# First layer of a hybrid mixer: normalisation applied after the transpose instead of before it

## Chip, cores and metric

The kernel runs on one core of one Trainium2 chip. The metric is the device time of one execution in microseconds (us); three runs of the kernel before have a median of 1519.49 (1518.29 to 1520.88). The engines are called by their short names: PE (TensorE, matrix products and transposes), DVE (VectorE), ACT (ScalarE), POOL (GpSimd) and SP (SyncE, which here only issues transfers).

## The reference

Two layers of a diffusion backbone over 512 tokens x and 256 context tokens, 1024 channels each. A layer normalises its tokens, modulates them with a scale and a shift that are products of a condition vector with a weight, projects the result h to 3840 channels for four mixers, and merges the mixers. The change concerns only how h of the first layer is made:

```python
def rmsnorm(x, gain):
    xf = x.astype(jnp.float32)
    y = xf * lax.rsqrt(jnp.mean(xf * xf, axis=-1, keepdims=True) + EPS)
    return (y * gain.astype(jnp.float32)).astype(x.dtype)
...
    for l in range(DEPTH):
        shift, scale, gate = jnp.split((silu_c @ w_mod[l] + b_mod[l])[:, None, :], 3, axis=-1)
        shift_c, scale_c, gate_c = jnp.split(silu_cc @ w_mod[l] + b_mod[l], 3)
        h = rmsnorm(x, norm_gain[l]) * (1.0 + scale) + shift
        hc = rmsnorm(xc, norm_gain[l]) * (1.0 + scale_c) + shift_c
        za, zb, zh, zf, zg = jnp.split(h @ w_in[l], SPLIT_IDX, axis=-1)
```

## The kernel before, in words

The 768 tokens (512 + 256) lie as six tiles of 128. For the projections, h is needed transposed: channels on partitions, 8 blocks of 128 channels by 768 tokens. Each fp32 value is held as a high part that PE multiplies at its fast rate and a low remainder (`h_hi`, `h_lo`; for weights `wh`, `wl`), and each product is three: high by high, high by low, low by high. The helper `split` makes such a pair: ACT rounds to the high part, DVE subtracts.

The function `opening` makes `h_hi` and `h_lo` of layer 0. The tokens come in eight transfers of 384 KB, `x[j, u]`: three token tiles (u = 0 or 1) by 256 channels (j = 0 to 3). ACT squares each, DVE sums the squares, and `rstd` forms the reciprocal root mean square by an integer first guess and three rounds of refinement, 13 tiny DVE instructions, once for u = 0 and once for u = 1. DVE scales the tokens in place, PE transposes them into two PSUM buffers (`psw`), and ACT copies the transposed blocks out. The modulation comes in eight pieces of 1 MB of `w_mod`, taken in four steps i, each with the shift piece i and the scale piece 4 + i for two of the eight blocks. For a piece, `mod_rows` multiplies the condition with it (`spread`, 16 instructions on PE, at 32 output rows), ACT copies the rows out (`mrow`), and `columns` turns them into per-channel columns with four PE instructions and one DVE copy; `mod_columns` adds bias and gain. Then DVE applies scale and shift to the blocks and `split` writes `h_hi` and `h_lo`.

The other stream is `Weights`: projection weights arrive in pieces of 512 KB in two raw buffers (`wraw`), ACT and DVE split them into `wh` and `wl` (four buffers each), and every pair of pieces serves one projection. The first projection, `hg_gates`, gives the forget gates of the recurrent mixer (HGRN2). Its four results (two halves of 128 columns, two ranges of 384 tokens) stand in two `psw` buffers, and its products are cut into groups of two channel blocks.

No order is written by hand. Every operation is recorded first; `Program.order` then plays the program with a price for each operation and issues, engine by engine, the one that could start earliest by these prices, ties going to the lower rank. Weight transfers and weight splits have their rank lowered by `AHEAD` (400). The engines then run their instructions strictly in that order, so an instruction that waits holds what stands behind it on its engine. All compute instructions have one line in the profile, L345, where the order is emitted; the tiles tell them apart.

Of the kernel before, what the change touches and what calls it, by code (L numbers as in the profile page):

```python
# [21 lines left out]
P = 128  # L22
# [3 lines left out]
NT = NX + NC  # L26
# [17 lines left out]
LEVELS = (64, 32, 16, 8, 4, 2, 1)  # L44
# [119 lines left out]
AHEAD = 400  # L164
# [185 lines left out]
def tile_hybrid_mixers(ctx, tc, io, out, dump=None):  # L350
# [6 lines left out]
    nc = Program()  # L357
# [21 lines left out]
    def psg():  # L379
        return pg.tile([P, 512], F32, tag="g", name=nm("psg"))  # L380
# [25 lines left out]
    def transpose(out, in_):  # L406
        nc.tensor.transpose(out, in_, ident)
# [6 lines left out]
    ident = kc[:, KC_ID:KC_ID + P]  # L414
    blk = kc[:, KC_BLK:KC_BLK + P]
    csel = kc[:, KC_SEL:KC_SEL + 2]
    rsel = [kc[:, KC_SEL + 2 + w:KC_SEL + 3 + w].to_broadcast([P, P]) for w in range(2)]
    masks = cpool.tile([P, len(LEVELS), P], I8, name="masks")

    hi_t = hpool.tile([P, 8, NT], F32R, tag="hhi", name="h_hi")  # L420
    lo_t = hpool.tile([P, 8, NT], F32R, tag="hlo", name="h_lo")

    def load_masks():
        for a, b in ((0, 4), (4, len(LEVELS))):
            mraw = slot([P, b - a, P], I32)
            nc.gpsimd.dma_start(mraw, io["masks"][:, a:b, :])
            nc.vector.tensor_copy(masks[:, a:b, :], mraw)


    sides, done, flags = [], set(), set()  # L430
# [33 lines left out]
    def rsqrt(v, n, size=None):  # L464
        small = lambda _, *a: _small(size or n, *a)[:, 0:n]
        i = small(n, "ri", 1, I32)
        nc.vector.tensor_scalar(i, v.bitcast(I32), 1, None, ALU.logical_shift_right)
        y0 = small(n, "ry", 1, I32)
        ts(y0, i, -1.0, RSQRT_MAGIC)
        y = y0.bitcast(F32)  # L470
        t = small(n, "rt", 1)
        for k in range(3):
            tt(t, y, y, ALU.mult)
            stt(t, t, -0.5, v, ALU.mult, ALU.mult)
            z = small(n, "rz", 3)
            stt(z, t, 1.5, y, ALU.add, ALU.mult)
            y = z
        return y

    def split(hi, lo, src):  # L480
        act(hi, src)
        tt(lo, src, hi.bitcast(F32), ALU.subtract)

    class Weights:
# [5 lines left out]
            self.raw, self.ready, self.work = [], [], None  # L490
            self.held = self.current = 0

        def fetch(self):
            while self.plan and len(self.raw) + bool(self.work) < RAW_BUFS:
                t = wpool.tile([P, 1024], F32, tag="wraw", bufs=RAW_BUFS, name=nm("wraw"))
                nc.ahead = AHEAD
                nc.sync.dma_start(t, self.plan.pop(0))
                nc.ahead = 0
                self.raw.append(t)
# [68 lines left out]
    weights = Weights(plan())  # L568
# [53 lines left out]
            nc.sync.dma_start(t[-1][:, 0:n, :], src[:, 256 * a:256 * (a + n)].rearrange("p (k c) -> p k c", c=256))  # L622
        return lambda k: t[k // 3][:, k % 3, :]

    def mod_rows(w):
        ps = psg()[:, 0:256]
        spread(ps, w, range(8))
        rows = sp.tile([P, 256], F32, tag="mrow", bufs=2, name=nm("mrow"))
        act(rows, ps)
        return rows  # L630

    def columns(tmp, j, rows):
        ps = psg()[:, 0:4]
        for b in range(2):
            mm(ps[:, 2 * b:2 * b + 2], rows[:, P * b:P * (b + 1)], csel)
        nc.vector.tensor_copy(tmp[:, j // 4, 2 * (j % 4):2 * (j % 4) + 2, :], ps.rearrange("p (k w) -> p k w", w=2))
# [10 lines left out]
    def opening():  # L647


        mc = cpool.tile([P, 2, 8, 2], F32, tag="modc", bufs=1, name=nm("modc"))  # L650
        tmp = small(32, "mt", 1).rearrange("p (a k w) -> p a k w", a=2, w=2)
        norm = Norm(None)
        x = {}
        for u in range(2):
            for j in range(4):
                x[j, u] = slot([P, 3, 256])
                nc.sync.dma_start(x[j, u], io["xin"][384 * u:384 * (u + 1), 256 * j:256 * (j + 1)].rearrange("(t p) d -> p t d", p=P))
        fetch = lambda i: [mod_fetch(io["w_mod"][0, j]) for j in (4 + i, i)]
        w = {0: fetch(0)}
        weights.fetch()  # L660
        for u in range(2):
            for j in range(4):
                sq = slot([P, 3, 256])
                act(sq, x[j, u], AF.Square)
                nc.vector.tensor_reduce(norm.ss[:, 3 * u:3 * u + 3, j], sq, AX.X, ALU.add)
            r = norm.rstd(3 * u, 3 * u + 3, 4)
            for j in range(4):
                tt(x[j, u], x[j, u], r.unsqueeze(2).to_broadcast([P, 3, 256]), ALU.mult)
        w[1] = fetch(1)
        xT = []  # L670
        for i in range(4):
            for k in (2 * i, 2 * i + 1):
                ps = psw()[:, 0:NT]
                for t in range(6):
                    transpose(ps[:, P * t:P * (t + 1)], x[i, t // 3][:, t % 3, P * (k % 2):P * (k % 2 + 1)])
                xT.append(slot())
                act(xT[k], ps)
        for i in range(4):
            for j, wj in zip((4 + i, i), w.pop(i)):
                columns(tmp, j, mod_rows(wj))  # L680
            mod_columns(0, mc, tmp, 2 * i, 2 * i + 2)
            for k in (2 * i, 2 * i + 1):
                for c, n0, n1 in ((0, 0, NX), (1, NX, NT)):
                    ts(xT[k][:, n0:n1], xT[k][:, n0:n1], mc[:, 0, k, c:c + 1], mc[:, 1, k, c:c + 1])
                split(hi_t[:, k, :], lo_t[:, k, :], xT[k])
            if i < 2:
                w[i + 2] = fetch(i + 2)
                for _ in range(4):
                    weights.pump()
# [35 lines left out]
    class Norm:  # L725
# [8 lines left out]
            act(junk, x, AF.Square, accum_out=self.ss[:, t, j:j + 1])  # L734

        def rstd(self, t0, t1, n):
            v = small(3, "sv", 1)
            m = t1 - t0
            nc.vector.tensor_reduce(v[:, 0:m], self.ss[:, t0:t1, 0:n], AX.X, ALU.add)
            ts(v[:, 0:m], v[:, 0:m], 1.0 / D, EPS)  # L740
            return rsqrt(v[:, 0:m], m, 3)

        def scale(self, t0, t1, n):

# [504 lines left out]
    def hg_mix(l, z, res):  # L1249
        full = l == 0  # L1250
        W = NT if full else NX
        nch = W // P
        yield from wait_for((l, "hf", 0))
        if full:
            load_masks()
        fl, om, dl = hg_bounds(l)
        gn = small(64, "hgn", 1)
        nc.gpsimd.dma_start(gn, io["smalls"][l:l + 1, SM_HGG:SM_HGG + 64].partition_broadcast(P).rearrange("p a d -> p (a d)"))
# [264 lines left out]
    mc = None  # L1523
# [80 lines left out]
def _constants():  # L1604
# [13 lines left out]
            kc[r, KC_SEL + w] = 1.0  # L1618
            kc[r, KC_SEL + 2 + w] = 0.5
    i = np.arange(P)  # L1620
    masks = np.zeros((P, len(LEVELS), P), np.int32)
    for n, L in enumerate(LEVELS):
        same = (i[:, None] // (2 * L)) == (i[None, :] // (2 * L))
        masks[:, n] = same & ((i[:, None] // L) != (i[None, :] // L))
# [85 lines left out]
```

## Time and profile before

| | us |
|---|---|
| median of three runs | 1519.49 |
| the profiled execution | 1520.19 |
| its span, first to last instruction | 1518.4 |
| PE busy in the span | 1457.1 |
| DVE busy | 953.6 |
| ACT busy | 628.5 |
| POOL busy | 106.7 |

A row of the timeline starts with the start in us from the beginning of the span and a duration; "x4" merges four like instructions, and the duration then runs from the first start to the last end. A row by forms gives, behind the bar, the busy time in us, the mean of one instruction in ns, and the idle time before them. A product is named by its output and inputs, the moving shape last: `psw<-h_hi,wh 128*128 128x384` is one of the three products of a weight tile with 384 tokens. Successive products overlap: they show 0.34 us each and start 0.17 apart. The granted clock of PE (PEclk) has two levels, 1.00 for 2.4 GHz and 0.50 for 1.2 GHz; a value between is a mean over both.

### The profile page before, as it was taken

Reading aid. Unit: us, or ns where it says so; the run is one execution under the profiler, and the core shown is the slowest. Engines: PE = TensorE matmul, PEld = TensorE weight load, DVE = VectorE, ACT = ScalarE, POOL = GpSimd, SP = SyncE. Lnnn points to the kernel's source line nnn. Section 1 sums busy time; section 2 is a strip of 40 time slices with the busy share of each in tenths; the row PEclk is TensorE's granted clock in tenths of the full one; section 3 lists DMA queues with packets and bytes.
Section 4 is the critical chain, followed back from the end, with each engine's and each line's share of the span. In section 5 each row is a group of like instructions: output and inputs, shape, how many; then the busy total and the mean of one; then the engine's idle time right before and its main releaser. Section 6 shows DMA issues by size and latency. Waiting matters only on the chain.

```text
span 1518.4 us, 25432 instructions
## 1 busy us (share of the span) xinstructions
PE 1457.1 (96%) x10068; PEld 1331.9 (88%) x10068; DVE 953.6 (63%) x2058; ACT 628.5 (41%) x1384; POOL 106.7 (7%) x207
## 2 busy tenths in 40 slices
PE   3999999999999997999999999999999999999998
PEld 2899989889999997889999999898887889888788
DVE  7794988577553355643444467979967855673544
ACT  5344454466522243431323244436445634552330
POOL 1000002210000010100001110000131000110000
PEclk9999999999999998999999999999999999999999
DMA  9211012332322142362222331211253222545332
GB/s 350 109 43 43 32 57 70 85 85 91 115 77 70 53 107 93 75 218 74 80 73 92 113 103 57 70 33 56 70 134 98 88 83 84 136 132 176 101 111 74
DMA packets 50599, 144.76 MB, mean 95 GB/s; under 512 B 7280, under 2 KB 12400, under 8 KB 50480
## 3 DMA queue, kind: packets, MB, share of 16 engines
q1 hardware_dynamic: 38336, 112.21, 22.7%
q0 software_dynamic: 12144, 30.93, 8.0%
q8 instruction: 79, 1.29, 0.3%
q14 instruction: 40, 0.33, 0.1%
HBM read 123.98 MB, written 4.19 MB: 84 GB/s over the span
## 4 chain that ended last, share of the span: by engine, by line
PE 85%; DVE 6%; ACT 5%; issue 2%; DMA 1%; SPq 0%; ACTq 0%; DVEq 0%; POOLq 0%
PE psg L345 69%; PE psw L345 11%; PE pst L345 4%; DVE u L345 3%; ACT u L345 3%; DVE sm L345 2%; ACT wh L345 1%; DMA u<-in_xin_dram 1%; ACT mth L345 0%; DVE wl L345 0%; DMA u<-in_rpb_dram 0%; DVE nss L345 0%; DVE psw L345 0%; SPq L345 0%; ACT h_hi L345 0%
## 5 line engine op out<-in xcount | busy, mean ns | idle before, releaser
L345 PE MATMUL psg<-h_hi,wh 128*128 128x384 f32 (+2 forms) x1216 | 439.6, 362 | 4.0 <-ACT mth L345 2.8
L345 PE MATMUL psg<-h_lo,wh 128*128 128x384 f32 (+2 forms) x1216 | 430.3, 354 | 0.2 <-DVE h_lo L345 0.2
L345 PE MATMUL psg<-h_hi,wl 128*128 128x384 f32 (+2 forms) x1216 | 430.4, 354 | 0.0
L345 DVE TENSOR_TENSOR wl<-wraw,wh 128x512 fp32r<-128x512 f32 x312 | 201.7, 686 | 175.8 <-ACT wh L345 174.9
L345 ACT ACTIVATE wh<-wraw 128x512 fp32r<-128x512 f32 x312 | 180.2, 624 | 244.7 <-PE psg L345 218.7
L345 PEld LDWEIGHTS psg<-h_hi,wh 128*128 128x128 f32 x1216 | 230.1, 189 | 24.9 <-ACT mth L345 5.7
L345 PEld LDWEIGHTS psg<-h_hi,wl 128*128 128x128 f32 x1216 | 229.8, 189 | 15.8
L345 PEld LDWEIGHTS psg<-h_lo,wh 128*128 128x128 f32 x1216 | 230.4, 189 | 14.8 <-DVE h_lo L345 0.5
L345 PE MATMUL psg<-wh,h_hi 128*128 128x256 f32 x544 | 156.3, 287 | 0.0
L345 PE MATMUL psw<-u,u 64*128 64x128 f32 (+6 forms) x1144 | 141.2, 299 | 12.3 <-ACT u L345 7.5
L345 PE MATMUL psg<-wl,h_hi 128*128 128x256 f32 x544 | 151.0, 278 | 0.0
L345 PE MATMUL psg<-wh,h_lo 128*128 128x256 f32 x544 | 150.9, 277 | 0.0
L345 ACT ACTIVATE u<-psw 128x768 f32<-128x768 f32 (+12 forms) x248 | 114.4, 485 | 81.3 <-PE psw L345 72.7
L345 PEld LDWEIGHTS psw<-u,u 64*128 64x128 f32 (+2 forms) x1144 | 113.1, 192 | 28.3 <-ACT u L345 13.2
L345 ACT ACTIVATE u<-psw,sm 128x768 f32<-128x768 f32 (+2 forms) x120 | 90.6, 758 | 88.9 <-DVE sm L345 75.7
L345 PE MATMUL psg<-wh,u 128*128 128x256 f32 x640 | 114.2, 280 | 0.9 <-ACT mth L345 0.9
L345 ACT ACTIVATE mth<-psg 128x384 f32<-128x384 f32 (+1 forms) x120 | 62.1, 519 | 127.8 <-PE psg L345 120.4
L345 DVE SCALAR_TENSOR_TENSOR mth<-mth,psg 128x384 f32<-128x384 f32 (+1 forms) x96 | 57.1, 595 | 91.0 <-ACT mth L345 73.9
L345 PE MATMUL psg<-u,wh 128*128 128x384 f32 (+1 forms) x384 | 107.6, 361 | 0.2 <-DVE u L345 0.2
L345 DVE TENSOR_REDUCE sm<-psw 128x1 f32<-128x768 f32 (+3 forms) x100 | 89.5, 901 | 26.1 <-PE psw L345 25.6
L345 PEld LDWEIGHTS psg<-wh,h_hi 128*128 128x128 f32 x544 | 102.2, 188 | 4.0
L345 POOL DMA_DIRECT2D u<-u x132 | 65.1, 505 | 568.8 <-ACT u L345 343.0
(128 smaller groups left out, 2002.9 us busy)
## 6 DMA issues: line engine op xcount, KB each, us to landing
wraw<-in_w_merge_dram SPq DMA_DIRECT2D x64, 512.0 KB, 3.6
wraw<-in_w_in_dram SPq DMA_DIRECT2D x60, 512.0 KB, 3.8
u<-in_w_mod_dram SPq DMA_DIRECT2D x32, 384.0 KB, 7.0
wraw<-in_w_up_dram SPq DMA_DIRECT2D x16, 512.0 KB, 3.5
wraw<-in_w_out_dram SPq DMA_DIRECT2D x16, 512.0 KB, 4.2
u<-u POOLq DMA_DIRECT2D x72, 96.0 KB, 2.4
u<-in_w_gate_dram SPq DMA_DIRECT2D x16, 384.0 KB, 6.3
u<-u POOLq DMA_DIRECT2D x24, 192.0 KB, 2.6
```

Source lines behind the costliest of these rows:

```text
L345: getattr(getattr(nc, engine), method)(*map(f, args), **{k: f(v) for k, v in kw.items()})
```

## The change

Tokens arrive ordered by channel range (j outside, u inside), the first two weight pieces come behind the first two modulation pieces (`weights.fetch(0)` leaves the rank alone), and the masks come as int8 in one transfer without a conversion. The tokens are transposed unscaled, DVE copies the blocks out, and ACT squares five of the eight transfers in narrow pieces with an accumulator. `rstd` is called once for all six tiles; a diagonal tile `dg` of the six columns, multiplied by a tile of ones, gives `R`, a row over the 768 tokens on all partitions. One SCALAR_TENSOR_TENSOR multiplies a block by scale and `R`, ACT adds the shift while it rounds to `h_hi`, and a second SCALAR_TENSOR_TENSOR adds the shift and subtracts `h_hi`. All modulation rows share one PSUM buffer, `pm`.

```diff
+    nc.gpsimd.dma_start(masks, io["masks"])
-    def load_masks():
-        for a, b in ((0, 4), (4, len(LEVELS))):
-            mraw = slot([P, b - a, P], I32)
-            nc.gpsimd.dma_start(mraw, io["masks"][:, a:b, :])
-            nc.vector.tensor_copy(masks[:, a:b, :], mraw)
...
-        weights.fetch()
-        for u in range(2):
-            for j in range(4):
-                sq = slot([P, 3, 256])
-                act(sq, x[j, u], AF.Square)
-                nc.vector.tensor_reduce(norm.ss[:, 3 * u:3 * u + 3, j], sq, AX.X, ALU.add)
-            r = norm.rstd(3 * u, 3 * u + 3, 4)
-            for j in range(4):
-                tt(x[j, u], x[j, u], r.unsqueeze(2).to_broadcast([P, 3, 256]), ALU.mult)
+        weights.fetch(0)
         w[1] = fetch(1)
         xT = []
-        for i in range(4):
-            for k in (2 * i, 2 * i + 1):
+        for j in range(4):
+            for u in range(2):
+                if 2 * j + u < 5:
+                    for t in range(3):
+                        norm.square(3 * u + t, j, x[j, u][:, t, :])
+                else:
+                    sq = slot([P, 3, 256])
+                    act(sq, x[j, u], AF.Square)
+                    nc.vector.tensor_reduce(norm.ss[:, 3 * u:3 * u + 3, j], sq, AX.X, ALU.add)
+            for k in (2 * j, 2 * j + 1):
...
-                act(xT[k], ps)
+                nc.vector.tensor_copy(xT[k], ps)
+        r = norm.rstd(0, 6, 4)
+        dg, ones, R = slot([P, 6, P]), slot([P, P]), slot()
+        nc.vector.memset(ones, 1.0)
+        tt(dg, ident.unsqueeze(1).to_broadcast([P, 6, P]), r.unsqueeze(2).to_broadcast([P, 6, P]), ALU.mult)
+        ps = psw()
+        mm(ps[:, 0:512], ones, dg[:, 0:4, :])
+        mm(ps[:, 512:768], ones, dg[:, 4:6, :])
+        act(R, ps[:, 0:NT])
+        pm = pst()
         for i in range(4):
             for j, wj in zip((4 + i, i), w.pop(i)):
-                columns(tmp, j, mod_rows(wj))
+                columns(tmp, j, mod_rows(wj, pm[:, 0:256]), pm[:, 256 + 4 * j:260 + 4 * j])
...
-                    ts(xT[k][:, n0:n1], xT[k][:, n0:n1], mc[:, 0, k, c:c + 1], mc[:, 1, k, c:c + 1])
-                split(hi_t[:, k, :], lo_t[:, k, :], xT[k])
+                    h, hi, lo = xT[k][:, n0:n1], hi_t[:, k, n0:n1], lo_t[:, k, n0:n1]
+                    stt(h, h, mc[:, 0, k, c:c + 1], R[:, n0:n1], ALU.mult, ALU.mult)
+                    act(hi, h, AF.Identity, bias=mc[:, 1, k, c:c + 1])
+                    stt(lo, h, mc[:, 1, k, c:c + 1], hi.bitcast(F32), ALU.add, ALU.subtract)
```

What the new recording does to the order is seen at three places. On DVE, before, near the end of the normalisation: `nss` holds the sums of squares, `sm` the columns of `rstd`, u_81 to u_91 are tokens.

```order
L345 TENSOR_REDUCE nss_141<-u_205 128x3
L345 TENSOR_TENSOR u_81<-u_81,sm_211 128x768
L345 TENSOR_TENSOR u_85<-u_85,sm_211 128x768
L345 TENSOR_TENSOR u_87<-u_87,sm_211 128x768
L345 TENSOR_TENSOR u_91<-u_91,sm_211 128x768
L345 TENSOR_REDUCE nss_141<-u_215 128x3
L345 TENSOR_REDUCE sm_230<-nss_141 128x3
```

On DVE now, at the same place; the COPY rows bring transposed blocks out of PSUM, u_214, u_239 and u_256 are the three wide squares.

```order
L345 COPY u_212<-psw_197 128x768
L345 TENSOR_REDUCE nss_110<-u_214 128x3
L345 COPY u_235<-psw_218 128x768
L345 COPY u_237<-psw_228 128x768
L345 TENSOR_REDUCE nss_110<-u_239 128x3
L345 TENSOR_REDUCE nss_110<-u_256 128x3
L345 COPY u_272<-psw_241 128x768
L345 TENSOR_REDUCE sm_274<-nss_110 128x6
```

The scalings are gone from between the reduces, and copies of blocks that were transposed unscaled stand there. On PE before, at the start of the first projection (`psw_491<-h_hi,wh_105`), behind the columns (`kc,mrow`) and the last spread (`u,cst`):

```order
L345 MATMUL psg_462<-kc,mrow_459 128x2 x2
L345 MATMUL psg_467<-kc,mrow_465 128x2 x2
L345 MATMUL psg_474<-u_189,cst 32x256 x3
L345 MATMUL psg_474<-u_232,cst 32x256 x3
L345 MATMUL psg_474<-u_239,cst 32x256 x2
L345 MATMUL psw_491<-h_hi,wh_105 128x384
L345 MATMUL psw_491<-h_lo,wh_105 128x384
L345 MATMUL psw_491<-h_hi,wl_110 128x384
```

On PE now, at the start of the same projection (`psw_368<-h_hi,wh_314`):

```order
L345 MATMUL pst_259<-u_136,cst 32x256 x3
L345 MATMUL pst_259<-u_147,cst 32x256 x3
L345 MATMUL pst_259<-u_151,cst 32x256 x2
L345 MATMUL psw_368<-h_hi,wh_314 128x384
L345 MATMUL psw_368<-h_lo,wh_314 128x384
L345 MATMUL psw_368<-h_hi,wl_320 128x384
...
L345 MATMUL pst_259<-kc,mrow_365 128x2 x2
L345 MATMUL pst_259<-u_153,cst 32x256 x3
L345 MATMUL pst_259<-u_164,cst 32x256 x3
L345 MATMUL pst_259<-u_170,cst 32x256 x2
```

The first products came behind the spreads of all eight pieces; now they come behind the third, and the other spreads stand between products. On DVE now, between the third and the fourth step; `wl_504`, `wl_523` and `wl_557` are low parts of weight pieces, `sm_303` the columns, `modc_341` the scale and shift:

```order
L345 TENSOR_TENSOR wl_504<-wraw_329,wh_492 128x512 x2
L345 SCALAR_TENSOR_TENSOR h_lo<-u_237,modc_341,h_hi 128x256
L345 TENSOR_TENSOR wl_523<-wraw_338,wh_515 128x512 x2
L345 COPY sm_303<-pst_259 128x4 x2
L345 TENSOR_TENSOR wl_557<-wraw_519,wh_547 128x512 x2
L345 TENSOR_TENSOR sm_303<-sm_303,cols 128x2x4
L345 SCALAR_TENSOR_TENSOR modc_341<-sm_303,cols 128x4
L345 COPY modc_341<-sm_303 128x4
L345 SCALAR_TENSOR_TENSOR u_272<-u_272,modc_341,u_334 128x512
```

Three pairs of low weight parts, the second to the fourth of which were not there before, stand ahead of the fourth step (u_272).

## Rows read from the trace of the kernel before

**Rows 1.** The page, 40 slices of the span, busy tenths of PE.
```profile
PE   3999999999999997999999999999999999999998
```
**Rows 2.** Table by stretches: us, busy time and instructions of each engine, clock, DMA.
```profile
0.00:48.00 48.00, 23.34 (x204) 15.12 (x204) 34.77 (x91) 24.21 (x38) 5.66 (x14) 0.96 0.95 340
48.00:100.00 52.00, 52.00 (x372) 50.17 (x370) 44.26 (x67) 19.45 (x35) 0.00 (x0) 0.97 0.12 41
```
**Rows 3.** Waits of PE: for whom, us in total, times, longest.
```profile
PE psg L345 <- DVE sm L345: 19.4, 1, 19.4
```
**Rows 4.** The chain that ended last, opening: start, us, what.
```profile
20.67 3.47 DVE u L345 x4
...
29.72 3.05 PE psw L345 x15
```
**Rows 5.** Timeline of PE, first products of the first two projections.
```profile
48.01 0.69 PE L345 MATMUL psw<-h_hi,wh 128*128 128x384 f32 x1
...
66.62 0.34 PE L345 MATMUL psg<-h_hi,wh 128*128 128x384 f32 x1
```
**Rows 6.** Timeline of ACT: the tanh, and a square with accumulator (layer 1).
```profile
6.82 0.22 ACT L345 ACTIVATE sm<-cols 128x16 f32<-128x16 f32 x1 [0.66 <-DMA cols<-in_cols_dram]
...
838.20 0.42 ACT L345 ACTIVATE sq<-u 128x256 f32<-128x256 f32 x1 [2.95 <-DVE u L345]
838.52 0.18 ACT L345 ACTIVATION_READ_ACCUMULATOR sq<-u 128x1 f32 x1
```
**Rows 7.** DVE by forms, whole span: busy us, mean ns, idle before.
```profile
L345 DVE TENSOR_REDUCE sm<-psw 128x1 f32<-128x768 f32 x64 | 60.4, 953 | 18.0 <-PE psw L345 17.9
L345 DVE TENSOR_TENSOR h_lo<-u,h_hi 128x768 fp32r<-128x768 f32 x8 | 7.4, 956 | 0.9 <-ACT h_hi L345 0.7
L345 DVE SCALAR_TENSOR_TENSOR mth<-mth,u 128x512 f32<-128x512 f32 x8 | 5.5, 690 | 0.1
L345 DVE TENSOR_SCALAR u<-u,modc 128x512 f32<-128x512 f32 x8 | 4.4, 544 | 0.1
L345 DVE SCALAR_TENSOR_TENSOR u<-u,sm,u 128x256 f32<-128x256 f32 x8 | 3.8, 480 | 0.1
L345 DVE TENSOR_SCALAR u<-u,modc 128x256 f32<-128x256 f32 x8 | 3.3, 408 | 0.0
L345 DVE SCALAR_TENSOR_TENSOR sm<-sm,sm 128x3 f32<-128x3 f32 x12 | 1.9, 160 | 0.3
```
**Rows 8.** ACT by forms, whole span.
```profile
L345 ACT ACTIVATE u<-psw 128x768 f32<-128x768 f32 x46 | 37.2, 811 | 24.0 <-PE psw L345 22.0 <-DVE u L345 1.6
L345 ACT ACTIVATE u<-u 128x768 f32<-128x768 f32 x37 | 31.3, 845 | 19.8 <-DVE u L345 14.9 <-DMA u<-in_xin_dram 4.1 <-DVE masks L345 0.3
```
**Rows 9.** PE: a spread and columns (timeline); fp32 products by form.
```profile
37.50 1.07 PE L345 MATMUL psg<-u,cst 128*32 128x256 f32 x16
39.21 0.51 PE L345 MATMUL psg<-kc,mrow 128*128 128x2 f32 x4
...
L345 PE MATMUL psg<-mrow,kc 128*128 128x256 f32 x24 | 6.5, 379 | 0.0
```
**Rows 10.** Table by stretches of 1 us; the clock is third from the end.
```profile
28.00:29.00 1.00, 0.00 (x0) 0.00 (x0) 0.86 (x6) 0.00 (x0) 0.00 (x0) 1.00 1.05 405
31.00:32.00 1.00, 1.00 (x7) 0.92 (x6) 1.00 (x2) 1.00 (x3) 0.00 (x0) 0.50 1.04 390
```
**Rows 11.** The page's DMA issues (KB, us to landing), and SP's timeline.
```profile
wraw<-in_w_in_dram SPq DMA_DIRECT2D x60, 512.0 KB, 3.8
u<-in_w_mod_dram SPq DMA_DIRECT2D x32, 384.0 KB, 7.0
...
20.94 14.68 SPq L345 DMA_DIRECT2D u<-in_w_mod_dram  x16
```
**Rows 12.** Timeline of DVE and PE where the recurrent mixer starts.
```profile
60.38 0.56 DVE L345 TENSOR_SCALAR u<-psw 128x384 f32<-128x384 f32 x1 [1.52 <-PE psw L345]
...
85.14 0.94 PE L345 MATMUL psw<-u,u 64*128 64x128 f32 x12
```

More of the change, by code (lines that the diff above doesn't have):

```diff
@@ L491, in __init__, with fetch @@
             self.held = self.current = 0
-        def fetch(self):
+        def fetch(self, ahead=AHEAD):
             while self.plan and len(self.raw) + bool(self.work) < RAW_BUFS:
                 t = wpool.tile([P, 1024], F32, tag="wraw", bufs=RAW_BUFS, name=nm("wraw"))
-                nc.ahead = AHEAD
+                nc.ahead = ahead
                 nc.sync.dma_start(t, self.plan.pop(0))
@@ L623, in mod_fetch, with mod_rows @@
         return lambda k: t[k // 3][:, k % 3, :]
-    def mod_rows(w):
-        ps = psg()[:, 0:256]
+    def mod_rows(w, ps=None):
+        ps = psg()[:, 0:256] if ps is None else ps
         spread(ps, w, range(8))
@@ L630, in mod_rows, with columns @@
         return rows
-    def columns(tmp, j, rows):
-        ps = psg()[:, 0:4]
+    def columns(tmp, j, rows, ps=None):
+        ps = psg()[:, 0:4] if ps is None else ps
         for b in range(2):
@@ L659, in opening @@
         w = {0: fetch(0)}
-        weights.fetch()
-        for u in range(2):
-            for j in range(4):
-                sq = slot([P, 3, 256])
-                act(sq, x[j, u], AF.Square)
-                nc.vector.tensor_reduce(norm.ss[:, 3 * u:3 * u + 3, j], sq, AX.X, ALU.add)
-            r = norm.rstd(3 * u, 3 * u + 3, 4)
-            for j in range(4):
-                tt(x[j, u], x[j, u], r.unsqueeze(2).to_broadcast([P, 3, 256]), ALU.mult)
+        weights.fetch(0)
         w[1] = fetch(1)
         xT = []
-        for i in range(4):
-            for k in (2 * i, 2 * i + 1):
+        for j in range(4):
+            for u in range(2):
+                if 2 * j + u < 5:
[6 more added lines that the diff above has]
+            for k in (2 * j, 2 * j + 1):
                 ps = psw()[:, 0:NT]
                 for t in range(6):
-                    transpose(ps[:, P * t:P * (t + 1)], x[i, t // 3][:, t % 3, P * (k % 2):P * (k % 2 + 1)])
+                    transpose(ps[:, P * t:P * (t + 1)], x[j, t // 3][:, t % 3, P * (k % 2):P * (k % 2 + 1)])
                 xT.append(slot())
-                act(xT[k], ps)
+                nc.vector.tensor_copy(xT[k], ps)
[8 more added lines that the diff above has]
+        pm = pst()
         for i in range(4):
             for j, wj in zip((4 + i, i), w.pop(i)):
-                columns(tmp, j, mod_rows(wj))
+                columns(tmp, j, mod_rows(wj, pm[:, 0:256]), pm[:, 256 + 4 * j:260 + 4 * j])
             mod_columns(0, mc, tmp, 2 * i, 2 * i + 2)
@@ L736, in rstd @@
         def rstd(self, t0, t1, n):
-            v = small(3, "sv", 1)
             m = t1 - t0
+            s = 6
+            v = small(s, "sv", 1)
             nc.vector.tensor_reduce(v[:, 0:m], self.ss[:, t0:t1, 0:n], AX.X, ALU.add)
             ts(v[:, 0:m], v[:, 0:m], 1.0 / D, EPS)
-            return rsqrt(v[:, 0:m], m, 3)
+            return rsqrt(v[:, 0:m], m, s)
         def scale(self, t0, t1, n):
@@ L1253, in hg_mix @@
         yield from wait_for((l, "hf", 0))
-        if full:
-            load_masks()
         fl, om, dl = hg_bounds(l)
@@ L1620, in _constants @@
     i = np.arange(P)
-    masks = np.zeros((P, len(LEVELS), P), np.int32)
+    masks = np.zeros((P, len(LEVELS), P), np.int8)
     for n, L in enumerate(LEVELS):
```

## The prediction

> **What bounds the kernel now.** I read first the 40 slices of the page: TensorE (PE) is at nine tenths nearly everywhere, and the first slice stands at 3 [rows 1]. The table by stretches says it in us: of the first 48.0 us PE is busy 23.3, and from 48 to 100 it is busy all 52.0 [rows 2]. Only the opening is loose, so that is where a change of the opening can earn, and what it earns stays as long as PE then runs without a gap. The list of waits names the first idle: PE has nothing for 19.4 us [rows 3]. The chain of waits says what the opening waits for: the tokens land, then VectorE (DVE) scales them (four scalings from 20.67, four more behind), then PE transposes from 29.72 [rows 4]. The timeline of PE gives my mark. The first projection product (128x384) starts at 48.01 and the ninety-seventh at 66.62, with no idle between [rows 2, 5]. I call six such products a unit; so 16 units are done at 66.6. If the changed kernel has 16 units done, and nothing more to wait for, at T, it gains 66.6 - T.
>
> **The change, step by step.** Names are those of the order's excerpts.
>
> *Squares.* ScalarE (ACT) begins them after its tanh on the condition, which waits for a small load until 6.82 and takes 0.22, so 7.0 [rows 6]. Now five of the eight are done as three narrow squares with an accumulator; one of these with its read takes 838.20 to 838.70, 0.50 [rows 6]. 15 x 0.51 = 7.7 end at 14.7, and three wide ones at 0.85 [rows 8], a little under that back to back, end at 15.5, 16.3 and 17.1. Token transfers lose two weight pieces (1.05 MB) in front of them and run at 340 GB/s [rows 2], so 3 us earlier: the last is in by about 15 and ACT is the limit.
>
> *From the squares to the row R.* Before the reduce of the sixth square DVE has nothing left, and behind it stand, in its order, three reduces, four copies of transposed blocks, 14 tiny instructions and the diagonal tile. No row has a copy of 128x768 out of PSUM on DVE; a reduce reading the same takes 0.95, ACT's copy 0.81 [rows 7, 8]. I take 0.95, less 0.08 of overlap (four of 0.95 take 3.47 in the chain [rows 4]): 7 x 0.87 = 6.1; tiny ones 0.16 [rows 7] and a gap, 0.2 x 14 = 2.8; the diagonal is 0.95 as the h_lo subtraction. 15.5 + 9.9 = 25.4. The two products that spread R (768 columns of plain fp32) are not in the trace; the nearest row is fp32 products of 256 columns, two instructions of 0.38 each [rows 9]: three of them are 2.3 without overlap, half of it with. PE will have idled some 3 us here; before, it idled from 28 to 29 and ran at half clock at 31 [rows 10], so I take 2.6: 28.0. R's eviction 0.8, 28.8. Beside it DVE makes four low weight halves (at 0.69 for 512 columns less overlap, 2.5) and PE the columns of the first modulation pieces (0.5 to 0.9, [rows 9]); four tiny DVE instructions follow: 29.8. What goes is eight scalings (3.47 twice) in front of the transposes, and ACT's eight copies.
>
> *The modulation steps.* A step (two blocks) was four TENSOR_SCALAR and two subtractions; now it is eight SCALAR_TENSOR_TENSOR. By rows of that kind, 0.69 for 512 columns and 0.48 for 256 [rows 7], 4 x 0.69 + 4 x 0.48 = 4.7; less overlap, the seven before PE's first unit take 3.8 and all eight 4.3, against 2 x (0.54 + 0.41) + 2 x 0.96 = 3.8, 3.5 with overlap. That is dearer by 0.8 a step. Bounds: 3.5 a step if they overlap as well as the old ones, 4.9 if not at all. The Trainium skill (VectorE: DVE Perf Modes, The perf-mode tier table) speaks against this edit: a one-source fp32 op in SBUF runs at twice the rate of one with two tensors. The rows show 0.69 against 0.54, not twice; by the rule the modulating half of a step would take 3.8 instead of 1.9, where I take 2.3, and with most of that in the path four times the gain below would shrink by 4 us.
>
> *Units between the steps.* In the new order PE does the units of a step as soon as it is made, between the spreads (1.07) and columns (0.51) [rows 9], instead of after all. First step: 29.8 + 3.8 = 33.6. Products start 0.17 apart, so a unit is 1.04 at full clock, twice that at half. One unit at half clock (1.9), columns, spread, one unit, columns: 38.7. DVE 0.8 of tiny ones and 3.8: the second step at 43.3. PE meanwhile spreads, two units, columns, spread to 43.7, a unit, columns: 45.2. Third step 45.2 + 0.8 + 3.8 = 49.8. Behind it on DVE stand four low halves (2.5) and the last h_lo: 52.6; on PE unit, columns, spread, unit, columns: 53.9. Now the added wait: DVE's order puts a third pair of low weight halves (wl_557) ahead of the fourth step. Its raw piece can be loaded only when the first of the two raw buffers is free, at 51.0, and lands 3.8 later [rows 11], 54.8; with both conversions 56.6. What queues behind it on DVE is the fourth step: 56.6 + 0.6 + 3.8 = 61.0, and for that PE waits: it has two units and four of the next weights, 53.9 to 60.1, then idles 0.9. T = 61.0, with 16 units done.
>
> *What is hidden.* The last modulation weights were issued by 35.6 and landed 7.0 later [rows 11], near 43; 1.4 MB less in front of them (two weight pieces and three quarters of the masks) is 4 us, so 39, where PE asks for them at 51: the transfers have left the path, and if they came back they would cost only what exceeds 12 us. The masks' two conversions go from DVE at a time when it now waits for squares: nothing. ACT's h_hi with a bias runs beside DVE: nothing while a step is DVE's.
>
> **Sum.** 66.6 - 61.0 = 5.6. I round down to 5 for what a hand walk leaves out. The profiled execution took 1520.2, 0.7 over the median of 1519.5; taken from the median, 1514.5. Ends of the unknown costs: a step at 4.9 and R late cost 3 us, all at the other end (full clock, no wl_557 wait) gives 3 more: gains of 2 to 8.
>
> **Behind the mark.** The first recurrent-branch work starts from the first gate block: DVE's second read of it was at 60.38, and PE took what DVE made of it at 85.14, without idle [rows 2, 12]. Now that block is done two units after T, at 63.1, so DVE's result comes 2.7 later, at about 88. PE's new order puts 96 products of 384 and 84 of 256 columns in front (16.6 us, and by columns 9.8), so it arrives at 87.4: they meet, with at most 1 us of idle.
>
> **Rivals.**
> *A. Half clock through the steps.* PE now alternates between short bursts and waits until 61; before, half clock followed an idle of under 3 us [rows 10]. Each unit then costs 0.9 more; of twelve, about five stand in the chain of steps: T = 65.5, gain 1, 1518.5. For it: PE is idle about a third of 34 to 50. Against: the 23 us of bursts in the first 48 before ran at a mean granted clock of 0.96 [rows 2].
> *B. The recurrent branch becomes the bound (slower).* DVE is nearly full after the mark. If its chain from the first gate block comes later than worked out (by 0.3 us a reciprocal or by a late weight half), PE waits at that product and at each of the products behind it; it decides from 6 us of lateness, and 9 us gives 1519.5 + 3.5 = 1523. For it: DVE starts 3 us later than before while PE is ahead. Against: other projections were put in between.
> *C. The gain is larger.* The fourth step isn't held (the raw piece is there earlier) and PE is warm: T = 57, gain 9 to 10, 1510. For it: transfers are ahead everywhere; against: DVE's 4.3 us a step is a floor.
> *D. The order behind the opening is dealt anew* for PE's next 1,700 instructions, and waits there grow or shrink by a few us either way; it widens all cases.
>
> **How the numbers follow.** Forecast (gain 2 to 8): 0.55; A, with what else eats the gain: 0.22; B: 0.11; C: 0.12. About 0.2% (3 us) is what a measurement can tell from no change. Faster by more: four fifths of the forecast, all of C, a tenth of A: 0.58. Slower: most of B and a little of A: 0.13. Same: 0.29. The range reaches from C's 1509 to 1521, just over the median before, and leaves out B.
>
> **What would show it.** Right: PE's first transpose near 8; the diagonal tile on DVE near 25; the first 128x384 product at 33 to 34, between spreads; the fourth step held on DVE by a weight half near 56; the ninety-seventh such product at 61, and PE full from there. Wrong: that product after 64 or before 58; a granted clock of 0.5 through 34 to 60 (A); PE waits on DVE between 85 and 130 (B); or a span that moved otherwise than that product did (D).

## The result and the profile after

The changed kernel is slower: 1532.09 us (1528.89 to 1533.14, four runs) against 1518.89 (1517.38 to 1520.88) for the kernel before on the same chip, ratio 1.0083, 95% interval 1.0063 to 1.0102. The forecast was 1514.5, a gain of 5; it is a loss of 13.

| | before | after |
|---|---|---|
| the profiled execution, us | 1520.19 | 1532.21 |
| span | 1518.4 | 1530.5 |
| first 128x384 product | 48.01 | 30.33 |
| ninety-seventh | 66.62 | 64.28 |
| PE busy in the span | 1457.1 | 1476.7 |

The two products of the changed kernel, in its timeline of PE:

```profile
30.33 0.69 PE L345 MATMUL psw<-h_hi,wh 128*128 128x384 f32 x1
...
64.28 0.34 PE L345 MATMUL psw<-h_hi,wh 128*128 128x384 f32 x1
```

Now the page after: busy tenths of PE and its granted clock in 40 slices.

```profile
PE   6999999999999997999999999999999999999999
...
PEclk8999999999999998999999999999999999999999
```

The first slice rose from 3 to 6 [rows 1], as meant, and no other slice fell. By the table PE idles 53.8 us of the span (61.3 before) and is busy 19.6 us longer: the lost time is no idle time. The table by stretches (columns as in [rows 2]) says the same of the opening, with the clock ahead of the DMA share:

```profile
0.00:48.00 48.00, 32.42 (x206) 22.90 (x210) 26.75 (x66) 19.66 (x54) 5.12 (x13) 0.83 0.88 312
48.00:100.00 52.00, 51.06 (x380) 47.77 (x373) 45.22 (x72) 22.81 (x43) 0.00 (x0) 0.99 0.19 61
...
36.00:38.00 2.00, 2.00 (x10) 1.80 (x7) 0.30 (x2) 0.38 (x1) 0.00 (x0) 0.50 1.03 397
...
46.00:48.00 2.00, 2.00 (x12) 1.90 (x14) 0.00 (x0) 0.00 (x0) 0.00 (x0) 0.50 0.03 8
```

PE has 9 us more in the first 48, part of it at half clock (mean 0.83, before 0.96). The list of waits of PE up to 310 us (for whom, total, times, longest) has lost the 19.4 us of [rows 3]; its four largest rows are now these:

```profile
PE psw L345 <- ACT u L345: 7.4, 9, 1.6
PE psw L345 <- DMA kc<-in_consts_dram: 7.3, 1, 7.3
PE psw L345 <- DVE u L345: 6.0, 4, 3.4
PE pst L345 <- ACT mrow L345: 1.8, 2, 1.3
```

From 309 us on the two kernels issue the same PE instructions in the same order, so equal products can be laid side by side. The timeline of before, then of after, at two of them:

```profile
309.30 0.52 PE L345 MATMUL psg<-h_hi,wh 128*128 128x384 f32 x1
...
1407.10 0.39 PE L345 MATMUL psg<-h_lo,wh 128*128 128x512 f32 x1
```

```profile
308.60 0.34 PE L345 MATMUL psg<-h_hi,wh 128*128 128x384 f32 x1
...
1417.93 0.39 PE L345 MATMUL psg<-h_lo,wh 128*128 128x512 f32 x1
```

At 309 the changed kernel is 0.7 us ahead; at 1407 it is 10.8 behind. The loss is made where nothing was changed, and it grows along the whole program. The groups of PE by form from 310 us on (busy us, mean ns of one), before and after:

```profile
L345 PE MATMUL psg<-h_hi,wh 128*128 128x384 f32 x631 | 216.7, 343 | 2.7 <-ACT mth L345 1.8 <-DVE mth L345 0.9
...
L345 PE MATMUL psg<-wh,h_hi 128*128 128x256 f32 x352 | 100.1, 284 | 0.0
```

```profile
L345 PE MATMUL psg<-h_hi,wh 128*128 128x384 f32 x629 | 217.2, 345 | 2.7 <-ACT mth L345 1.8 <-DVE mth L345 0.9
...
L345 PE MATMUL psg<-wh,h_hi 128*128 128x256 f32 x352 | 101.6, 289 | 0.0
```

The waits in these rows are the same; one product takes 2 to 5 ns longer. What can do that to untouched instructions? The tile pools give each kind of tile its address at its first use in the emitted order. A new order in the opening therefore moved nearly every tile in SBUF and in PSUM: `wh` from 122752 to 130368, `h_hi` from 159168 to 163264, `psg` from banks 0 to 2 to banks 5 to 7.

### The profile page after: what moved, and what is told of

It is laid out like the page before. It is cut to its first block, busy times and chain, and to the rows that moved or that the text cites. A ratio compares the mean times of both kernels' runs of the same rounds, so it can differ in the third digit from the quotient of the medians.

```text
span 1530.5 us, 25440 instructions
## 1 busy us (share of the span) xinstructions
PE 1476.7 (96%) x10072; PEld 1346.4 (88%) x10072; DVE 950.9 (62%) x2048; ACT 627.5 (41%) x1410; POOL 106.4 (7%) x206
## 4 chain that ended last, share of the span: by engine, by line
PE 84%; DVE 7%; ACT 5%; issue 2%; DMA 1%; SPq 0%; ACTq 0%; DVEq 0%; POOLq 0%
PE psg L345 69%; PE psw L345 10%; PE pst L345 5%; DVE u L345 4%; ACT u L345 3%; DVE sm L345 2%; ACT wh L345 1%; DMA u<-in_xin_dram 1%; DVE wl L345 0%; DVE h_lo L345 0%; ACT mth L345 0%; DMA u<-in_rpb_dram 0%; DMA wraw<-in_w_in_dram 0%; ACT sq L345 0%; DVE psw L345 0%
## 5 line engine op out<-in xcount | busy, mean ns | idle before, releaser
L345 PE MATMUL psw<-u,u 64*128 64x128 f32 (+7 forms) x1148 | 144.4, 303 | 18.4 <-ACT u L345 10.7
L345 ACT ACTIVATE u<-psw 128x768 f32<-128x768 f32 (+10 forms) x241 | 108.5, 475 | 71.9 <-PE psw L345 62.6
```

The costliest lines, as they stand in the source:

```text
L345: getattr(getattr(nc, engine), method)(*map(f, args), **{k: f(v) for k, v in kw.items()})
```

## The experiments

A kernel with other places gets these lines where the order is emitted; they ask the pools for all tiles in the order of a list, ahead of their use. With the list as it comes, addresses and order are those of the kernel itself. The other edits are lines that change `keys`.

```diff
+        first = {}
+        for op in order:
+            for t in op.tiles:
+                first.setdefault((t.space, t.tag), t)
+        keys = [k for k in first if k[0] != "dram"]
+        ...
+        for k in keys:
+            t = first[k]
+            for n in range(t.bufs):
+                pools[t.space].tile(t.shape, t.dt, tag=t.tag, bufs=t.bufs, name=f"place_{t.tag}_{n}")
```

To compare prices I read three stretches of products that all kernels issue alike, from the first start to the last in the timeline: 97 recorded products of 128x512 near 1390 us; 228 of 128x256 near 1255, counted from the start of the 128x512 product just ahead of them; 108 of 128x384 near 724. They repeat to 0.02 us. "Distance" is the start of `h_hi` less that of `wh`, modulo 256 bytes; it is the same for `h_lo` and `wl`, since these tiles lie multiples of 256 apart.

| run | kernel | distance | 128x512, us | 128x256 | 128x384 | ratio to before, 95% |
|---|---|---|---|---|---|---|
| | before | 64 | 21.97 | 25.99 | 18.63 | 1 |
| | after | 128 | 22.39 | 27.17 | 18.92 | 1.0063 to 1.0102 |
| e1 | after | 64 | 21.99 | 26.96 | 18.64 | 0.9995 to 1.0013 |
| e2 | before | 0 | 21.81 | 27.46 | 18.64 | 1.0046 to 1.0074 |
| e3 | after | 128 | 22.40 | 27.16 | 18.93 | 1.0068 to 1.0096 |
| e4 | after | 64 | 21.99 | 26.97 | 18.64 | 0.9985 to 1.0003 |
| e5 | after | 64 | 21.98 | 25.99 | 18.64 | 0.9982 to 1.0002 |
| e6 | before | 128 | 22.40 | 27.17 | 18.92 | 1.0099 to 1.0130 |
| e7 | before | 128 | 22.30 | 27.17 | 18.91 | 1.0060 to 1.0097 |
| e8 | after | 128 | 22.39 | 27.16 | 18.92 | 1.0064 to 1.0101 |
| e9 | after | 128 | 22.40 | 27.47 | 18.91 | 1.0065 to 1.0091 |
| e10 | before | 128 | 22.40 | 27.47 | 18.91 | 1.0075 to 1.0101 |
| e11 | before | 192 | 22.39 | 26.97 | 18.63 | 1.0048 to 1.0083 |
| e12 | after | 64 | 21.98 | 25.98 | 18.63 | 0.9985 to 1.0009 |
| e13 | before | 64 | 21.99 | 26.96 | 18.64 | 0.9996 to 1.0013 |
| e14 | after | 64 | 21.98 | 25.98 | 18.63 | 0.9976 to 0.9993 |
| e15 | before | 32 | 22.39 | 27.10 | 18.99 | 1.0047 to 1.0076 |
| e16 | before | 96 | 22.40 | 27.17 | 18.99 | 1.0081 to 1.0114 |
| e17 | after | 64 | 21.99 | 25.98 | 18.63 | 0.9973 to 0.9992 |
| e18 | before | 160 | 22.48 | 27.46 | 18.98 | 1.0065 to 1.0100 |

The 128x256 stretch without that first step, in before and then in the changed kernel:

```profile
1255.06 0.28 PE L345 MATMUL psg<-wh,h_hi 128*128 128x256 f32 x1
...
1280.82 0.28 PE L345 MATMUL psg<-wh,h_lo 128*128 128x256 f32 x1
```

```profile
1263.05 0.28 PE L345 MATMUL psg<-wh,h_hi 128*128 128x256 f32 x1
...
1289.98 0.28 PE L345 MATMUL psg<-wh,h_lo 128*128 128x256 f32 x1
```

For the same 227 steps that is 25.76 and 26.93 us.

### Is it the weights' place or the PSUM banks?

e1, in the changed kernel, wh and wl first of all:

```diff
+        w = [("sb", "wh"), ("sb", "wl")]
+        keys = w + [k for k in keys if k not in w]
```

> The changed kernel with one edit: the two weight buffers wh and wl are given their places in SBUF first, so that each partition's part begins at a multiple of 128 bytes (16512 and 32896) as in the kernel before, not 64 bytes behind one (130368 and 146752). Everything else keeps its offset within 128 bytes, PSUM banks are those of the changed kernel. Theory S (the start of wh and wl within 128 bytes sets the spacing of the products that read them): 1514 to 1516 us, spacing of the 128x256 products of w with h_hi or u back from 121.8 to about 117.9 ns, of the 128x384 products from 177.9 to about 175.5. Theory B (the PSUM banks of the accumulators set it): 1532, spacing as in the changed kernel. Theory C (another tile's place, or something run-wide): 1532.

e2, in the kernel before, the two in front of `mrow` (`w` as in e1):

```diff
+        keys = [k for k in keys if k not in w]
+        i = keys.index(("sb", "mrow"))
+        keys[i:i] = w
```

> The kernel before with one edit: wh and wl begin 64 bytes behind a multiple of 128 (124096 and 140480) and every other tile keeps its place within 128 bytes and its PSUM banks. Theory S: slower than before by what the changed kernel lost behind 310 us and more, 1533 to 1538 us, spacing of the 128x256 products up from 117.9 to about 121.8 ns. Theory B: 1519, no change. Theory C: 1519, no change.

e3, in the changed kernel, the PSUM tags in before's order (`"g w t"`); e4, this and the edit of e1:

> The changed kernel with one edit: PSUM banks as in the kernel before (the accumulators psg in banks 0 to 2, psw in 3 and 5, pst in 7, instead of psg 5 to 7, psw 0 and 2, pst 4); SBUF as in the changed kernel. Theory S: 1532, no change. Theory B: 1514 to 1516, spacing of the products as in the kernel before. Theory C: 1532.

> The changed kernel with both edits: wh and wl at multiples of 128 bytes and the PSUM banks of the kernel before. Theory S: 1514 to 1516, as with the weights alone. Theory B: 1514 to 1516, as with the banks alone. Theory C: 1532. If the two causes add, the two runs with one edit lie between and this one is at 1514 to 1516.

Measured: e1 1519.0, e2 1528.1, e3 1530.8, e4 1517.6. The banks do nothing (theory B falls). Moving the weights alone takes the loss away in one kernel and makes most of it in the other, as theory S said. Its sizes did not come out: it had e1 and e4 at 1514 to 1516 and e2 at 1533 to 1538. And e2 grew only in the 128x256 stretch, which theory S did not foresee.

### All places exchanged

e5 and e6 have the other kernel's list of keys, so the two orders and the two sets of places stand crossed.

> The changed kernel with every tile, in SBUF and in PSUM, at the address that it has in the kernel before; the order of the instructions is the changed kernel's. It shows what the change is worth by itself. Theory S (places alone make the slowdown): the 12 us lost behind 310 us are gone, spacing of the products as before (128x256 117.9, 128x384 175.5, 128x512 229.7 ns), and what the opening gained at the ninety-seventh product stays (3.7 us in the run with the weights moved): 1514 to 1516. Theory C (something of the new order itself makes the products slower): 1519 or more, spacing over 119 and 176.

> The kernel before with every tile, in SBUF and in PSUM, at the address that it has in the changed kernel; the order of the instructions is that of before. Theory S: the places alone cost 14 to 17 us, so 1532 to 1536, spacing as in the changed kernel (128x256 121.8, 128x384 177.9, 128x512 232.5 ns). Theory C: 1518, spacing as before.

The pages' lines for PE: the kernel before, e5 (changed order, places of before), e6 (order of before, changed places), and the changed kernel.

```profile
PE 1457.1 (96%) x10068; PEld 1331.9 (88%) x10068; DVE 953.6 (63%) x2058; ACT 628.5 (41%) x1384; POOL 106.7 (7%) x207
```

```profile
PE 1460.2 (96%) x10072; PEld 1332.4 (88%) x10072; DVE 950.4 (63%) x2048; ACT 627.3 (41%) x1410; POOL 106.5 (7%) x206
```

```profile
PE 1476.3 (96%) x10068; PEld 1348.3 (88%) x10068; DVE 953.9 (62%) x2058; ACT 629.0 (41%) x1384; POOL 106.9 (7%) x207
```

```profile
PE 1476.7 (96%) x10072; PEld 1346.4 (88%) x10072; DVE 950.9 (62%) x2048; ACT 627.5 (41%) x1410; POOL 106.4 (7%) x206
```

PE's busy time follows the places (16 to 19 us), not the order (3 us and less). In time: e6 takes 1536.5, 18 more than before, e5 1517.7, 0.4 less (theory S had e5 at 1514 to 1516). The places alone make the slowdown.

### Which property of the places?

e7 moved the weights of before to 126272 (distance as after, 64 behind a multiple of 128 as in e2), e8 those of the changed kernel by 4 KB. In `keys`, e7 takes everything between `wl` and `h_hi` but the 128 bytes `sm16` ahead of `wh`; e8 takes `mth` behind `wl`.

> The kernel before, with wh at 126272 and wl at 142656: again 64 bytes behind a multiple of 128, as in the run with only the weights moved (124096), but now h_hi begins 32896 bytes behind wh, which is the distance in the changed kernel (there 130368 and 163264); the other tiles keep their offset within 128 bytes. In the run with 124096 only the 128x256 products grew, and 128x384 and 128x512 hardly (176.4, 228.9). Theory distance (w and h a multiple of 16 KB and 128 bytes apart slow the products with w stationary): 128x384 to 178, 128x512 to 232.5 ns, 1532 to 1534. Theory offset alone: as the run with 124096, 1528. Theory raw pieces (wraw at 96 bytes behind a multiple of 128 takes part): 1528.

> The changed kernel with one buffer pair (mth) placed behind the weights instead of ahead of them: wh at 126272, wl at 142656, still 64 bytes behind a multiple of 128, wraw still at 96, but h_hi now 36992 bytes behind wh instead of 32896. Theory distance: 128x384 and 128x512 back to 175.5 to 176.4 and 229 to 230 ns, 128x256 stays at 122 to 123, so 1522 to 1526. Theory raw pieces or offset alone: 177.9 and 232.5, 1532.

e7 is slow (1530.5) in all three stretches, e8 too (1531.1): the 16 KB don't matter, and `wraw` doesn't (at 0 in e7, at 96 in e8). Both have 128 as the distance modulo 256. I had not yet seen that, and tried offsets first: e9 and e10 move `cols` behind `u` and `ftf1` ahead of `h_hi`, e11 `sm16` ahead of `wh`.

> The changed kernel with the addresses of before, but two small buffers moved so that h_hi and h_lo begin at a multiple of 128 bytes (159232 and 183808, not 64 behind one) and the work buffers u too (25856, not 96 behind one); wh and wl stay at 122752 and 139136. If the offset of every tile that TensorE reads counts as that of wh and wl did: products with h as the moving side shorten by about what they lost with wh at 126272 (2.5 to 3 ns of 175.7 and 230.1), 8 to 12 us in all: 1506 to 1510. If only wh and wl count: 1515 to 1518, as with the addresses of before.

> The kernel before with the same two moves: h_hi, h_lo and u at multiples of 128 bytes as wh and wl. If every operand's offset counts: 1507 to 1511. If only wh and wl count: 1518. The difference to the changed kernel at the same addresses is what the change itself is worth, 1 to 4 us.

> The kernel before with wh and wl 128 bytes further on (122880 and 139264), so at multiples of 256 bytes; before they are 128 behind one. So far: 128 behind a multiple of 256 (122752, 16512) gives 118 and 175.5 ns, 192 behind one (124096) 123.0 and 176.4, 64 behind one (126272, 130368) 121.9 and 178. Theory offset in 128 bytes: 118 and 175.5 ns, 1518. Theory offset in 256 bytes (or more): another price, unknown to both sides, 1510 to 1536.

1531.4, 1532.1 and 1528.7: e9 and e10 missed on both readings. With every operand at a multiple of 128 bytes they are slow, so an offset by itself is not it. By the distance (128, 128, 192) all runs so far fall in order. e13 and e14 keep 64 with offsets that no run had had; e15, e16 and e18 set others.

```diff
e13  + "... hgn64 ftf1 gss12 wh wl sm16 ..."       both 128 bytes further on
e14  + "... wh wl mt32 modc ftf1 hhi hlo ..."      wh 128 back, h_hi 64 on
e15  + "... hgn64 sv3 wh wl ..."                   wh 32 on
e16  + "... modc nlam1 hhi hlo ..."                h_hi 32 on
e18  + "... modc nlam1 ftf1 hhi hlo ..."           h_hi 96 on
```

> The kernel before with two small buffers moved ahead of the weights, so that wh, wl, h_hi and h_lo all begin 128 bytes further on (122880 and 139264, 159296 and 183872): their offsets within 256 bytes are new (0 and 64; before 128 and 192), their distance from each other is that of before (36416, which is 64 beyond a multiple of 256). With w alone moved by 128 it took 1528.7. Theory distance: 1518, spacing as in the kernel before (118, 175.5, 229.7 ns). Theory offsets: 1528 to 1536.

> The changed kernel in its own layout but for two small buffers: one of 128 bytes behind the weights instead of ahead of them, one of 64 ahead of h_hi instead of behind h_lo. So wh begins at 130240 and h_hi at 163328 (offsets within 256 bytes 192 and 0, neither that of before), 33088 apart, which is 64 beyond a multiple of 256 as in the kernel before; in the changed kernel it is 32896, 128 beyond one. Everything else lies within 128 bytes of where the change put it. Theory distance: 1516 to 1519, spacing 118, 175.5, 229.7 ns. Theory offsets: 1531.

> The kernel before with one buffer of 32 bytes moved ahead of the weights: w 32 bytes further on, h where it was, their distance 32 beyond a multiple of 256 instead of 64. Theory distance: between the prices of 0 (123.0, 176.4, 228.9 ns; 1528) and 64 (118, 175.5, 229.7; 1518), unless 64 is not the best, when it is under 1518. Theory offsets: no forecast, 1510 to 1536.

> The kernel before with one buffer of 32 bytes moved ahead of h_hi: h 32 bytes further on, w where it was, their distance 96 beyond a multiple of 256. Theory distance: between the prices of 64 (1518) and 128 (1531), unless 64 is not the best, when it is under 1518. Theory offsets: no forecast, 1510 to 1536.

> The kernel before with h_hi and h_lo 96 bytes further on, w where it was: distance 160 beyond a multiple of 256. Theory distance: slow as 128 and 192 are, 1528 to 1532, 128x512 at 232 to 233 ns. If only some distances collide and this is none: 1518 or less.

e13 takes 1519.1 and e14 1515.9; e15, e16 and e18 take 1528.4, 1532.2 and 1530.9. The theory of distance holds in both kernels, but its forecast of prices between the neighbours' did not: e15's 128x512 stretch (22.39) is over those of 0 and of 64. In e15, e16 and e18, though, `wh` or `h_hi` also starts 32 bytes off a multiple of 64, which happens in no other run, and their 128x384 stretch (18.98 to 18.99) has a price of its own (elsewhere 18.63 to 18.64 or 18.91 to 18.93). So that offset may count by itself: it is not shown that 32, 96 and 160 are slow as distances. With both tiles at multiples of 64 only 0, 64, 128 and 192 are possible; 0 and 192 were tried in one run each, and only 64 is ever fast in all three stretches. The timeline of e14, first and last of the 97 products of 128x512, then the same two of e6:

```profile
1389.69 0.40 PE L360 MATMUL psg<-u,wl 128*128 128x512 f32 x1
...
1411.67 0.39 PE L360 MATMUL psg<-h_hi,wl 128*128 128x512 f32 x1
```

```profile
1407.67 0.40 PE L360 MATMUL psg<-u,wl 128*128 128x512 f32 x1
...
1430.07 0.39 PE L360 MATMUL psg<-h_hi,wl 128*128 128x512 f32 x1
```

21.98 against 22.40 us, for the same instructions. e14, two small buffers away from the changed kernel, is faster than both kernels: ratio 0.9984 (0.9976 to 0.9993).

The 128x256 stretch has a second condition that distance doesn't tell: with 64 it is 25.98 or 25.99 in before, e5, e12, e14 and e17 but 26.96 or 26.97 in e1, e4 and e13; with 128 it is 27.16 to 27.17, but 27.47 in e9 and e10. What it hangs on was not found. In the 128x512 stretch e7 is the one exception, with 22.30 where the other runs at 128 have 22.39 or 22.40.

### What holds the opening back?

The prediction's rival A, at the places of before:

```diff
         ps = psw()
+        for t in range(24):
+            transpose(ps[:, 128 * (t % 6):128 * (t % 6 + 1)], x[3, t % 2][:, t % 3, 0:P])
         mm(ps[:, 0:512], ones, dg[:, 0:4, :])
```

> The changed kernel at the addresses of before, with 24 more transposes of 128x128 whose result nobody reads, on TensorE between the last spread before R's products and these, where it idled 3.7 us and went over to half clock until about 40. They leave no work out. If the half clock from 24.8 to 39.9 is what holds the opening back (the rival A of the prediction): granted clock 1.0 there, the two products of R in 1.4 instead of 2.7 to 2.9, the second modulation step from 40.2 to about 34, the ninety-seventh 128x384 product from 63.2 to 59 or earlier, 1511 to 1515. If the fourth step waits for its weight half whatever comes before: the second step is earlier, the ninety-seventh product stays at 62 to 63 and the time at 1516 to 1518.

It took 1517.9, the same as e5. Its timeline of PE, from the added transposes to the first projection product:

```profile
22.92 2.84 PE L360 MATMUL psw<-kc,u 128*128 128x128 f32 x24
25.60 1.46 PE L360 MATMUL psw<-u,u 128*128 128x512 f32 x4
...
32.03 1.01 PE L360 MATMUL pst<-kc,mrow 128*128 128x2 f32 x4 [3.64 <-ACT mrow L360]
32.97 1.93 PE L360 MATMUL pst<-u,cst 128*32 128x256 f32 x16
34.84 0.69 PE L360 MATMUL psw<-h_hi,wh 128*128 128x384 f32 x1
```

The spread products of `R` ran at full clock (1.46 for 2.68), but 24 added operations dealt the order anew, PE waited 3.64 us behind them, and the half clock came then. It was moved, not removed, so A is not decided by this run. The second step began hardly earlier (40.37 on DVE, 41.23 in e5), the ninety-seventh product at 63.8 (63.19 in e5).

e17 is e14 with the third weight pair behind the fourth step's start on DVE:

```diff
-            nc.ahead = AHEAD
+            self.count = getattr(self, "count", 0) + 1
+            nc.ahead = -40 if self.count in (5, 6) else AHEAD
```

> The changed kernel with the distance from w to h restored (as e14), and one number more: the conversion of the third weight pair isn't put 400 places ahead in the order but 40 behind, so that the low halves that stood in front of the fourth modulation step on VectorE now stand behind that step's first two SCALAR_TENSOR_TENSOR. Only 8 rows of TensorE's order differ. If the held fourth step sets the end of the opening: that step's first STT from 59.6 to about 57, the ninety-seventh product from 63.1 to 60 or 61, 1513 to 1515. If something else is late next (the third pair itself, which the next products need): ninety-seventh product 62 to 64, 1516 to 1518.

The step did start earlier, at 57.9 (DVE's timeline), and then stood behind the weight half for which it had made room:

```profile
57.91 1.15 DVE L360 SCALAR_TENSOR_TENSOR u<-u,modc,u 128x512 f32<-128x512 f32 x2
59.63 1.29 DVE L360 TENSOR_TENSOR wl<-wraw,wh 128x512 fp32r<-128x512 f32 x2 [0.58 <-ACT wh L360]
60.84 1.14 DVE L360 SCALAR_TENSOR_TENSOR h_lo<-u,modc,h_hi 128x512 fp32r<-128x512 f32 x2
```

Its ninety-seventh product starts at 66.00, 2.9 later than in e14 (63.09) and later than either reading had it, and yet it takes 1516.2 (ratio 0.9973 to 0.9992), which can't be told from e14. So the mark of the prediction does not measure the end to a few us.

## Why the prediction was wrong

**The step that failed** is in its first part: "what it earns stays as long as PE then runs without a gap". PE did run nearly without one: it idled 0.9 us from 48 to 100 and 0.3 from 85 to 130. What failed is the price of its products, which was taken as given by the instruction. It hangs on how far apart the two tiles lie that a product reads, and the change moved them. No term of the sum stood for that; it cost 14 to 18 us, where the sum was about 5. Of the signs that were named as wrong, one caught it: a span that moved otherwise than the ninety-seventh product did. It was put to an order dealt anew (rival D), but from 309 us on the order is the same.

**The gain of the opening** was real. In one pair of profiles it is smaller than forecast at the mark: with the places of before (e5) the ninety-seventh product starts at 63.19, a gain of 3.4 (2.3 in the changed kernel, at 64.28); forecast were 61.0 and 5.6. But the mark moves from run to run. In the ten profiles that keep the old order, whatever the places, it lies between 66.62 and 69.50, in the eight that keep the new one (all but e12 and e17) between 62.78 and 65.07. The 66.62 from which the forecast counted is at the early end of its ten. From median to median (68.48 to 63.37) the gain is 5.1; that this is near 5.6 is in part luck, as both ends lie about 2 us behind those of the forecast.

**"It gains 66.6 - T"** did not hold either, the places apart. At the first of the products laid side by side above (309.30 in before) the runs at distance 64 stand at 309.30 and 307.98 (e13) in the old order and at 306.04, 305.14, 306.66 and 305.71 (e1, e4, e5, e14) in the new, about 2.8 apart in the mean. From there to the last product the old order takes 1205.0 and 1206.0, the new 1203.4 to 1207.8. So of some 5 us at the mark about half is left at 309, and e17 moved the mark by 2.9 without moving the end. What takes the other half is open.

By steps, in the changed kernel:

- Diagonal: begun at 23.63 (forecast 24.4 to 25.4). `R` took 2.68 (forecast 2.6). Both stood.
- First product: 30.33, not 33.6. I let PE wait for seven of the step's instructions; it needed only the first SCALAR_TENSOR_TENSOR (STT) and ACT's high half, 1.6 us.
- A step of DVE: seven instructions from 28.77 to 32.70, 3.9 (forecast 3.8). The rows of a 512 and a 256 STT against [rows 7]:

```profile
L345 DVE SCALAR_TENSOR_TENSOR u<-u,modc,u 128x512 f32<-128x512 f32 x8 | 6.0, 748 | 0.0
...
L345 DVE SCALAR_TENSOR_TENSOR u<-u,modc,u 128x256 f32<-128x256 f32 x8 | 3.8, 479 | 0.0
```

  So 0.75 and 0.48, where one source took 0.54 and 0.41. Back to back three take 1.81. By the Trainium skill (VectorE: DVE Perf Modes, The perf-mode tier table) the factor would be two; these rows show 1.4 and 1.2.
- Third step: here the term was mis-sized. Its columns were to be done at 45.2; DVE got them at 49.47. PE waited 1.3 for a `mrow` and ran at half clock again from 46 to 48, and DVE's copy began only behind the spread of 1.6 that PE put after the columns. (The 43.7 on the way to 45.2 is 43.4 by its own terms.)
- Fourth step: held by the third pair of low weight halves, as forecast, but to 61.0 instead of 56.6, for the raw buffer came free with the late third step. DVE after, from its columns on:

```profile
58.11 0.16 DVE L345 COPY sm<-pst 128x4 f32<-128x4 f32 x1 [1.24 <-PE pst L345]
59.69 1.29 DVE L345 TENSOR_TENSOR wl<-wraw,wh 128x512 fp32r<-128x512 f32 x2 [1.42 <-ACT wh L345]
...
61.30 1.81 DVE L345 SCALAR_TENSOR_TENSOR u<-u,modc,u 128x512 f32<-128x512 f32 x3
```

**What reached the end** at equal places, by the ratios: e5 gains 1.2 us on before (2.7 to a loss of 0.3), e9 1.5 on e10, the changed kernel 4.9 on e6 (two series, 1.0083 and 1.0115), e1 and e4 0.0 and 1.5 on e13, whose stretches have the same prices. With the distance restored, e14 gains 2.4 (1.1 to 3.6). So the change by itself is worth about 0 to 5 us, mostly under the 5 forecast; only e14 and the pair with e6 are clear of noise. Its places cost 14 (against e5) to 18 (e6).

**Rivals.** A: half clock from about 25 to 39 and again at 46 did come, and the products and spreads there ran at it; how much of the late mark it makes, no run settles. B: from 85 to 130 PE is busy 44.7 of 45.0; it did not happen. C: no, the fourth step was held. D: between the mark and 309 us the orders differ, and e5's lead goes from 3.4 to 2.6 (309.30 against 306.66). That may be part of what the opening's gain lost on the way; it has no part in the loss behind 309.

## What to carry to other kernels

When a change alters which tile is allocated first, compare the addresses too, and compare the two kernels at equal addresses before anything is said on the change. A mark read from one profile moved by up to 2.9 us between runs of one order; take it from several before a few us are counted from it. If every product is some ns slower and no wait has grown, look at the distance between the tiles that a product reads. Pin the places of the large operand tiles rather than leave them to the order of first use.

## What was not expected of the hardware

In this program the cost of an fp32r product hangs on the distance from its weight tile to its token tile modulo 256 bytes: 64 against 128 is 228.9 against 233.3 ns for a 128x512 step (21.97 and 22.40 us by 96), 174.1 against 176.8 for 128x384 (18.63 and 18.92 by 107), 113.5 against 118.6 for 128x256 (25.76 and 26.93 by 227). The slow runs take 10 to 18 us more of 1518 over this program. At 0 only the 128x256 products suffer, at 192 these and the 128x512 (one run each). Multiples of 128 bytes for every operand do not help (e9, e10). The distance is not the whole of it: the 128x256 stretch has its second condition, and a tile 32 bytes off a multiple of 64 may cost by itself. That the weight load and the moving stream get in each other's way in SBUF would fit, since PEld is busy 88% beside PE, but no run shows that mechanism.

The Trainium skill (SBUF — State Buffer, SBUF: two separate sides) speaks against such a price: PE's port there never waits for anyone. The Trainium skill (the same page, A bandwidth-pool intuition that's wrong) gives weight loads a second, independent read port. The stretches above differ by up to 5.7% (25.99 and 27.47 us) with the instructions unchanged and only addresses moved; the measurement decides that the place counts, whatever the way.
